# Weight sums on VectorE and by accumulating DMAs in the second feed-forward product

## The chip, the cores and the metric

The kernel runs on one core of a Trainium2 chip. The metric is the device time of one execution in microseconds (us). Five engines work side by side, each through its own queue of instructions in order: TensorE (PE in the profile, its weight loads PEld), VectorE (DVE), ScalarE (ACT), GpSimd (POOL) and SyncE (SP). SP does nothing here but issue DMA transfers. GpSimd issues some as well, among them the ones that add what they bring to what lies at their destination ("accumulating" transfers, `accum_op=OP.add`).

## The reference

One layer of a decoder over 2048 tokens of width 1024, in float32: a normalised input goes through one projection, two mixers (gated linear attention and dilated attention) and an output projection; then comes the part that matters here, a feed-forward block of width 4096 and a last normalisation.

```python
        mixed = jnp.concatenate([o_a, o_b], axis=-1).astype(h.dtype)
        h = h + jnp.einsum('bsm,md->bsd', mixed, w_out[l])

        nm = rmsnorm(h, mlp_norm_g[l])
        a = jnp.square(jax.nn.relu(jnp.einsum('bsd,df->bsf', nm, w_ff1[l])))
        h = h + jnp.einsum('bsf,fd->bsd', a, w_ff2[l])
    return rmsnorm(h, final_norm_g)
```

## The kernel before

**How a product is made.** A float32 product is made of three matmuls in a faster format: every operand is split into a high part, which ScalarE copies, and a low part, which VectorE subtracts (`split`, lines 485 to 487; the name of the split operand tells which one it is), and high x high, low x high and high x low are summed in PSUM (`mm3`, lines 141 to 144). One matmul is 128 x 128 by 512 columns.

**FF1**, the first feed-forward product, runs twice over 16 pairs of column blocks, first for one half of the tokens, then for the other. It uses a scheme of seven block products in place of eight (`product1`); a job is one of them, 224 in all, and `prep1` splits its weights two jobs ahead (`w1comb`). The token operands of the seven products (`hb`) are held split in SBUF. While the last seven jobs of the first half run (from job `first` = 105), those of the second half are brought in: `reload` loads 1 MB (tile `rb`, from `hTD`) and splits it in two halves, one per job or so (line 1606 is the call, the splits are line 486 on ScalarE and 487 on VectorE). The first two loads are issued at job 103, each later one when the first half of the load two before it has been split. The results go through a squared ReLU and, added and subtracted in many combinations, to memory (`actD`).

**FF2**, the second, is a scheme of 26 block products (`PRODUCTS`, lines 75 to 100). Each line of the table says which weight blocks make up its right operand, and after the bar to which output blocks the result is added. A product has four steps, one for each quarter of the operand, and a step is 24 matmuls; step n belongs to product n // 4. For its right operand the kernel keeps a weight state (`bs`, four quarters of 512 KB), which goes from product to product: "=" loads a block into the quarter (SP, line 1497), "+" and "-" add and subtract a block. `fetch_b(n)` brings the blocks to be added or subtracted into one of four half tiles (`rb`, SP, line 1487); `update_b(n)` adds them into the quarter (line 1499), the first on GpSimd, a second on VectorE. The four steps prepared while FF1 ends use VectorE for both. `prep_b(n)` then splits the quarter into one of three buffers (`cb`, line 486 on ScalarE, 487 on VectorE), and `prep_a(n)` does so for the activations (`ca`, loaded by SP as `ra`, 1 MB for two steps; products with sign -1 take lines 1458 and 1459 instead). Per step, the loop asks for the update four steps ahead, the fetch six ahead, both splits two ahead, then for the 24 matmuls.

A finished product's four PSUM banks are taken during the next product's steps (`taken`): the first contribution to an output block is copied by ScalarE, the others are added by VectorE (line 1556). The residual `h` is added to the output blocks by 16 accumulating transfers of 512 KB on GpSimd's queue (`begin`, line 1544, from `hD`; the table `RESIDUAL` says with which product). When a block row is complete, after products 20, 23, 24 and 25, `output` normalises its four tiles: ScalarE sums squares, GpSimd multiplies the first half by the weights g (line 1517), VectorE scales and multiplies the second half (line 1520), ScalarE scales the first (line 1521), and SP stores both.

**Order.** In FF1 and FF2 the framework's scheduler decides the order of instructions on each engine, from dependencies and its own estimates of time; on the chip every queue then runs in that order.

Of the kernel before, what the change touches and what calls it, by code (L numbers as in the profile page):

```python
# [13 lines left out]
AF = mybir.ActivationFunctionType  # L14
OP = mybir.AluOpType
# [101 lines left out]
def emit(tc, a, stop=99):  # L117
    nc = tc.nc
    V, A, G, T, SP = nc.vector, nc.scalar, nc.gpsimd, nc.tensor, nc.sync
# [6 lines left out]
    def ps(tag):  # L126
        return psum.tile([128, 512], F32, name="ps_" + tag, tag=tag, bufs=BANKS[tag])

    def slot(name, dt=F32, n=SLOT):

        return up.tile([128, SLOT], dt, name=name, tag="u", bufs=25)[:, :n]

    def view(t, shape):
        n = int(np.prod(shape))
        names = "abcd"[:len(shape)]
        return t[:, :n].rearrange(f"p ({' '.join(names)}) -> p {' '.join(names)}", **dict(zip(names, shape)))
# [29 lines left out]
    def stat(n=1):  # L166
        if stat_at[0] + n > 48:
            stat_at[0] = 0
        s = stats[:, stat_at[0]:stat_at[0] + n]
        stat_at[0] += n  # L170
        return s

    def rstd_of(ssq, width, n=1, bias=eps):
        r = stat(n)
        A.activation(r, ssq, AF.Ln, bias=bias, scale=1.0 / width)
        A.activation(r, r, AF.Exp, scale=-0.5)
        return r
# [46 lines left out]
    hTD = dram.tile([2, 7, 128, 4, 512], F32, name="hTD")  # L224
# [15 lines left out]
    CX, c11, c12, c21, c22, last = [t[:, GP * q:GP * q + GP] for t in acc for q in range(2)]  # L240
# [11 lines left out]
    order = (1, 2, 5, 6, 3, 4, 7)  # L252
# [4 lines left out]
    TF = {j: [slot(f"tb{j}", FR) for _ in range(2 if j < 7 else 1)] for j in order}  # L257
# [227 lines left out]
    def split(hi, lo, src):  # L485
        A.activation(hi, src, AF.Copy)  # L486
        V.tensor_tensor(lo, src, hi.bitcast(F32), op=OP.subtract)  # L487
# [109 lines left out]
    def reload(n):  # L597

        j, cs = order[n // 2], slice(1024 * (n % 2), 1024 * (n % 2) + 1024)
        t = (xp, bp)[n // 2 % 2][:, cs]  # L600
        SP.dma_start(t, nTD[j - 1].rearrange("p c s -> p (c s)")[:, cs])

        def rest():
            hi, lo = [v[:, cs] for v in TF[j]]
            tc.keep_in_program_order(A.activation(hi, t, AF.Copy))
            V.tensor_tensor(lo, t, hi.bitcast(F32), op=OP.subtract)
            if n + 4 < 14:
                back.append(reload(n + 4))

        return rest  # L610
# [121 lines left out]
    for at in range(7, len(jobs)):  # L732
        g = jobs[at][0]
# [419 lines left out]
    for pr in range(4):  # L1153
# [3 lines left out]
        for hh, br in seq:  # L1157
            b = Branch()
            b.h, b.br = 2 * pr + hh, br
            m = 4 if br == 2 else 2  # L1160
            first = len(units)
# [62 lines left out]
    rb, TF, TB = [slot("rb")], {}, {}  # L1224
# [53 lines left out]
    order = (1, 2, 6, 5, 7, 3, 4)  # L1278
# [10 lines left out]
    def prep1(at):  # L1289

        if at >= len(jobs1):
            return
        g, j = jobs1[at]
        if not combs1:
            combs1.extend(view(c[:, 1024 * q:], (2, 4, 128)) for c in [slot("w1comb", FR) for _ in range(2)]
                          for q in range(2))
        r = raw1[g % 2]
        (a11, a12), (a21, a22) = [[r[:, 4 * k:4 * k + 4, n * 128:n * 128 + 128] for k in range(2)] for n in range(2)]
        c = combs1[at % 4]
        split(c[:, 0], c[:, 1], {1: a11, 2: a12, 6: a11, 5: a21, 7: a11, 3: a12, 4: a22}[j])  # L1300
        if j == 1:
            V.tensor_tensor(a21, a21, a22, op=OP.add)
            V.tensor_tensor(a11, a21, a11, op=OP.subtract)
        if j == 2:
            V.tensor_tensor(a12, a12, a11, op=OP.subtract)
        if j == 6:
            V.tensor_tensor(a11, a22, a11, op=OP.subtract)
        if j == 4:
            load_w1(g + 2)
# [80 lines left out]
    def some_sums(n=3):  # L1390

        for _ in range(n):
            while sums1 and next(sums1[0], 0) == 0:
                sums1.pop(0)
# [5 lines left out]
    for at, t in enumerate(tiles):  # L1400
        u, m = nxt
# [7 lines left out]
        p = [ps("a"), ps("a")]  # L1409
        parts_ = 2 if at < 2 else 1  # L1410
        for q in range(parts_):
            for n in range(2):
                cs = slice(n * 512, n * 512 + 512)
# [20 lines left out]
    raw_a, comb_a, raw_b, comb_b, state, fin = [], [], [], [], [], {}  # L1434
# [5 lines left out]
    def load_a(n):  # L1440

        if n < 2 * NPH:
            p, k = divmod(n, 2)
            if len(raw_a) < 2:
                raw_a.append(view(slot("ra"), (4, 512)))
            SP.dma_start(raw_a[n % 2], actD[AT[p], :, 4 * k:4 * k + 4].rearrange("p q h s -> p q (h s)"))
# [16 lines left out]
    fetched = {}  # L1463

    def w2_part(n, k, m):

        first = 8 * (n % 4) + 2 * (k % 2) + k // 2
        return w2[:, first:first + 5:4, 512 * m:512 * m + 512]

    def state_of(n):  # L1470

        if len(state) < 2:
            state.extend(view(slot("bs"), (4, 512)) for _ in range(2))
        return state[n % 4 // 2][:, n % 2 * 2:n % 2 * 2 + 2]

    def fetch_b(n):

        if n >= LAST:
            return
        if not raw_b:  # L1480
            raw_b.extend(view(v[:, 1024 * e:], (2, 512)) for v in [slot("rb2") for _ in range(2)] for e in range(2))
        fetched[n] = []
        for op, k, m in PRODUCTS[n // 4][2]:
            if op != "=":
                v = raw_b[turns[0] % 4]
                turns[0] += 1
                SP.dma_start(v, w2_part(n, k, m))
                fetched[n].append((op, v))

    def update_b(n, engines=(G, V)):  # L1490

        if n >= LAST:
            return
        v = state_of(n)
        for op, k, m in PRODUCTS[n // 4][2]:
            if op == "=":
                SP.dma_start(v, w2_part(n, k, m))
        for e, (op, r) in enumerate(fetched.pop(n)):
            engines[e].tensor_tensor(v, v, r, op=OP.add if op == "+" else OP.subtract)  # L1499

# [9 lines left out]
    def output(C, row, i, last=False):  # L1510

        scr = fin["scr"][:, 512 * (i % 2):512 * (i % 2) + 512]
        ss, part = stat(2), stat()
        for n in range(2):
            A.activation(scr, C[n], AF.Square, accum_out=ss[:, n:n + 1])
            if n == 0:
                G.tensor_tensor(C[0], C[0], fin["g"][:, :512], op=OP.mult)
                A.activation(part, ss[:, 0:1], AF.Copy, bias=EPS, scale=1.0 / D)
        r = rstd_of(ss[:, 1:2], D, bias=part)
        V.scalar_tensor_tensor(C[1], C[1], r, fin["g"][:, 512:], op0=OP.mult, op1=OP.mult)  # L1520
        A.activation(C[0], C[0], AF.Copy, scale=r)
        SP.dma_start(out2[row:row + 128, 512:], C[1])
        (A if last else SP).dma_start(out2[row:row + 128, :512], C[0])

# [58 lines left out]

    first, parts_at = 7 * (NP - 1), {}
    for n in range(14):
        parts_at.setdefault(first + 1 + n * 4 // 5, []).append(n // 2)
    halves, begun = {}, set()
    for at in range(7, len(jobs1)):
        if at == first - 2:
            halves.update({n: reload(order[n], 1) for n in range(2)})  # L1590
        prep1(at + 2)
        some_sums()
        product1(at)
        for n in parts_at.get(at, ()):
            next(halves[n])
            if n in begun and n + 2 < 7:
                halves[n + 2] = reload(order[n + 2], 1)
            begun.add(n)
        n = at + 6 - len(jobs1)
        if n == 0:  # L1600
            load_a(0)
        if 0 <= n < 4:
            fetch_b(n)
            update_b(n, (V, V))
        if n == 3:
            load_a(1)
        if n in (3, 5):
            prep_b(n // 2 - 1)
            prep_a(n // 2 - 1)
            fetch_b(n // 2 + 3)  # L1610

    some_sums(99)
    held2 = [None, None]
# [1 line left out]
    for ph, (_, chained, _, _) in enumerate(PRODUCTS):  # L1615
        if not chained:
            held2[ph % 2] = [ps(t) for t in ("acdc", "adco")[ph % 2]]
        P = held2[ph % 2]
        for k in range(4):
            n = 4 * ph + k  # L1620
            update_b(n + 4)
            if n + 6 not in fetched:
                fetch_b(n + 6)
            prep_a(n + 2)
            prep_b(n + 2)
            if k == 1:
                begin(ph)
            if left:
                taken(ph - 1, k, left[k])
            if ph < NPH - 1 or k < 2:  # L1630
                for c in range(2):
                    for i in range(4):
                        mm2(P[i], n, c, i, not chained)
        left = P
# [60 lines left out]
```

## Time and profile before

| | |
|---|---|
| median of 3 runs | 2280.32 us (2277.76 to 2281.45) |
| profiled execution, own time | 2283.21 us |
| its span | 2281.4 us |
| mean granted TensorE clock | 0.994 |
| TensorE busy | 2249.2 us (99%) |
| VectorE busy | 1630.4 us (71%) |
| ScalarE busy | 1230.4 us (54%) |
| GpSimd busy | 544.3 us (24%) |
| FF2's first weight split | 1678.9 us from the span's start |

The profile is of one execution. A row of its groups gives source line, engine, operation, output<-input with partitions x elements and type, the count, then total busy time, mean duration in ns, and how long the engine was idle just before, with what ended most of that time. In a timeline the first two numbers are start and duration in us, and the bracket is the idle time before, with its releaser. A row for one tile gives minimum, median and maximum duration in ns and the first and last start.

### The profile page before, as it was taken

How to read it: one execution, taken by the hardware profiler on the slowest of the kernel's cores; microseconds unless marked ns; L12 is line 12 of the kernel's file. 1: busy time of each engine (PE TensorE's matmuls, PEld its weight loads, DVE VectorE, ACT ScalarE, POOL GpSimd, SP SyncE). 2: the span in 40 equal slices, each digit the busy share in tenths (PEclk: the TensorE clock that was granted, in tenths of full speed). 3: DMA queues.
4: the chain of work that ended last, by engine and by line, in shares of the span. 5: the costliest groups of instructions: out<-in, count | busy, mean ns of one | idle time of the engine just before them, and what ended most of it. 6: DMA issues, size and time to landing. Idle time of an engine off the chain costs nothing.

```text
span 2281.4 us, 35136 instructions
## 1 busy us (share of the span) xinstructions
PE 2249.2 (99%) x12508; PEld 1945.9 (85%) x12508; DVE 1630.4 (71%) x3065; ACT 1230.4 (54%) x2436; POOL 544.3 (24%) x482
## 2 busy tenths in 40 slices
PE   9999999999999999999999999999999999999998
PEld 8978998899999998888888887888888878888876
DVE  8788878766667676446777778777777577576778
ACT  6665436426877874234555556555555433333446
POOL 1210002024385672000000000000007562032465
PEclk9999999999999999999999999999999999999999
DMA  5458754776768864678544456555479988676775
GB/s 201 134 182 245 252 155 136 223 234 221 223 196 255 262 207 139 221 232 273 185 138 153 137 161 202 163 165 163 128 266 285 311 279 277 214 254 227 261 255 175
DMA packets 359920, 478.59 MB, mean 210 GB/s; under 512 B 19333, under 2 KB 268694, under 8 KB 347712
## 3 DMA queue, kind: packets, MB, share of 16 engines
q1 hardware_dynamic: 355246, 467.69, 63.6%
q0 software_dynamic: 4352, 8.39, 2.0%
q8 instruction: 98, 1.61, 0.3%
q14 instruction: 78, 0.64, 0.1%
q10 hardware_dynamic: 146, 0.27, 0.0%
HBM read 326.54 MB, written 154.44 MB: 211 GB/s over the span
## 4 chain that ended last, share of the span: by engine, by line
PE 84%; DMA 5%; POOL 3%; DVE 3%; issue 3%; ACT 2%; SPq 0%; POOLq 0%; ACTq 0%; DVEq 0%
PE ps_a L143 9%; PE ps_a L142 9%; PE ps_a L144 9%; PE ps_c L143 7%; PE ps_c L142 7%; PE ps_c L144 7%; PE ps_a L893 4%; PE ps_o L142 3%; PE ps_o L144 3%; PE ps_o L143 3%; PE ps_d L143 3%; PE ps_d L142 3%; PE ps_d L144 3%; PE ps_d L874 3%; PE ps_c L852 2%
## 5 line engine op out<-in xcount | busy, mean ns | idle before, releaser
L1499 POOL TENSOR_TENSOR bs<-bs,rb 128x1024 f32<-128x1024 f32 x72 | 217.7, 3031 | 1072.3 <-DMA actD<-ring 836.9
L486 ACT ACTIVATE cb<-bs 128x1024 fp32r<-128x1024 f32 x104 | 110.2, 1060 | 272.7 <-issue 116.2
L487 DVE TENSOR_TENSOR cb<-bs,cb 128x1024 fp32r<-128x1024 f32 x104 | 165.2, 1589 | 124.4 <-ACT cb L486 123.7
L487 DVE TENSOR_TENSOR w1comb<-w1raw,w1comb 128x512 fp32r<-128x512 f32 x224 | 153.8, 689 | 96.4 <-ACT w1comb L486 95.5
L486 ACT ACTIVATE w1comb<-w1raw 128x512 fp32r<-128x512 f32 x224 | 140.3, 628 | 81.6 <-PE ps_c L144 29.5
L865 ACT ACTIVATE pe<-pe,O 128x256 f32<-128x256 f32 (+1 forms) x384 | 156.5, 453 | 45.8 <-DVE O L864 42.3
L893 PE MATMUL ps_a<-v,pt 128*128 128x65 f32 x1200 | 178.5, 253 | 2.5 <-ACT pt L881 1.9
L893 PEld LDWEIGHTS ps_a<-v,pt 128*128 128x128 f32 x1200 | 175.4, 196 | 3.5 <-ACT pt L881 2.1
L874 PE MATMUL ps_d<-ident,pe 128*128 128x128 f32 x600 | 159.7, 279 | 0.0
L864 DVE CUSTOM_DVE_ANT_0 pe<-ps_c,nb 128x256 f32<-128x256 f32 (+1 forms) x384 | 126.3, 361 | 40.9 <-PE ps_d L874 18.3
L286 ACT ACTIVATE wcomb<-wraw 128x512 fp32r<-128x512 f32 (+2 forms) x119 | 90.0, 757 | 98.8 <-PE ps_a L143 34.5
L142 PE MATMUL ps_c<-hb,w1comb 128*128 128x512 f32 x336 | 131.0, 390 | 0.5 <-ACT xs L1371 0.5
L143 PE MATMUL ps_c<-hb,w1comb 128*128 128x512 f32 x336 | 130.9, 390 | 0.0
L144 PE MATMUL ps_c<-hb,w1comb 128*128 128x512 f32 x336 | 130.2, 390 | 0.0
L487 DVE TENSOR_TENSOR ca<-ra,ca 128x1024 fp32r<-128x1024 f32 x84 | 126.8, 1511 | 3.8 <-ACT ca L486 3.8
L142 PE MATMUL ps_c<-cb,ca 128*128 128x512 f32 x312 | 122.1, 391 | 0.0
L143 PE MATMUL ps_c<-cb,ca 128*128 128x512 f32 x312 | 122.0, 391 | 0.0
L144 PE MATMUL ps_c<-cb,ca 128*128 128x512 f32 x312 | 122.0, 391 | 0.0
L351 POOL TENSOR_TENSOR acc<-acc,misc 128x264 f32<-128x264 f32 (+1 forms) x32 | 38.7, 1221 | 313.1 <-DMA wraw<-w_in 200.3
L874 PEld LDWEIGHTS ps_d<-ident,pe 128*128 128x128 f32 x600 | 110.0, 187 | 0.1
L142 PE MATMUL ps_a<-wo,mT 128*128 128x512 f32 x256 | 101.4, 396 | 0.0
L1362 ACT ACTIVATE acc<-acc 128x512 f32<-128x512 f32 x96 | 60.7, 632 | 74.1 <-DVE acc L1381 44.0
(410 smaller groups left out, 7146.7 us busy)
## 6 DMA issues: line engine op xcount, KB each, us to landing
ra<-actD SPq DMA_DIRECT2D x52, 1024.0 KB, 7.3
actD<-ring SPq DMA_DIRECT2D x176, 256.0 KB, 2.5
rb<-w_ff SPq DMA_DIRECT2D x88, 512.0 KB, 6.1
bs<-w_ff SPq DMA_DIRECT2D x72, 512.0 KB, 6.1
w1raw<-w_ff SPq DMA_DIRECT2D x32, 1024.0 KB, 5.7
k<-kD SPq DMA_DIRECT2D x16, 1024.0 KB, 7.4
rb<-hTD SPq DMA_DIRECT2D x13, 1024.0 KB, 5.9
wraw<-w_in SPq DMA_DIRECT2D x48, 256.0 KB, 3.9
```

The costliest lines, as they stand in the source:

```text
L142: T.matmul(out, sh, mh, start=first, stop=False, **kw)
L143: T.matmul(out, sl, mh, start=False, stop=False, **kw)
L144: T.matmul(out, sh, ml, start=False, stop=last, **kw)
L286: A.activation(hi, src, AF.Copy, scale=sc)
L486: A.activation(hi, src, AF.Copy)
L487: V.tensor_tensor(lo, src, hi.bitcast(F32), op=OP.subtract)
L864: V.tensor_tensor_reduce(p, s, bias, scale=1.0, scalar=BIG, op0=OP.add, op1=OP.min, accum_out=nm)
L865: A.activation(p, p, AF.Exp, bias=nm, scale=-1.0)
L874: T.transpose(pb[:, i * 128:i * 128 + 128], src, ident)
L893: T.matmul(self.b.opsum[:, n % 4], self.pt[:, i * 128:i * 128 + 128], self.b.v[:, blk, cols], start=first, stop=last)
L1362: A.activation(v, v, AF.Relu)
L1499: engines[e].tensor_tensor(v, v, r, op=OP.add if op == "+" else OP.subtract)
```

## The change

1. `update_b` uses VectorE alone: no weight sum is left on GpSimd. From step 16 on, "+" blocks are not fetched into `rb` at all; an accumulating transfer on GpSimd's queue adds them from memory to the state. Of 88 sums, 72 on GpSimd and 16 on VectorE, 52 remain, all on VectorE (12 "+" of the first four products and 40 "-"), and 36 become accumulating transfers: four each in products 4, 6, 8, 9, 16, 18, 21, 23 and 25. SP issues 52 block fetches in place of 88; the 72 "=" loads stay. Where a line of the table has both, the accumulating transfer comes before the subtraction.
2. In `output`, for 15 of the 16 tiles the first half is scaled and multiplied by VectorE in one instruction, as the second half is, in place of GpSimd's product and ScalarE's scaling.
3. The reload for the second half of the tokens is cut into 14 pieces of 512 KB. Four are issued one job earlier than the first two loads were, and piece n + 4 is issued once piece n has been split.
4. In FF2 the update is asked for three steps ahead in place of four, and the fetch five in place of six; before the loop, three updates are made in place of four.

In the order that the scheduler makes, VectorE has 2851 instructions in place of 2799, ScalarE 1897 in place of 1909, GpSimd 227 in place of 274 and SP 842 in place of 873 (waits left out). GpSimd's queue then holds the residual transfers and the weight transfers in turn: the first two residual blocks, the transfers of steps 16 and 17, one of the next residual block, that of 18, and so on; those of steps 32 to 39 alternate with six residual transfers, and those of steps 64 and later have no residual transfers among them. On VectorE, after product 7, stand the splits of step 29, the sum of step 32 (which waits for its transfer), four PSUM additions, the sum of 33, the splits of 30 and 31, the sum of 34 and the splits of 32.

```diff
@@ -1481,13 +1481,13 @@
             raw_b.extend(view(v[:, 1024 * e:], (2, 512)) for v in [slot("rb2") for _ in range(2)] for e in range(2))
         fetched[n] = []
         for op, k, m in PRODUCTS[n // 4][2]:
-            if op != "=":
+            if op == "-" or op == "+" and n < 16:
                 v = raw_b[turns[0] % 4]
                 turns[0] += 1
                 SP.dma_start(v, w2_part(n, k, m))
                 fetched[n].append((op, v))
 
-    def update_b(n, engines=(G, V)):
+    def update_b(n, engines=(V, V)):
 
         if n >= LAST:
             return
@@ -1495,6 +1495,8 @@
         for op, k, m in PRODUCTS[n // 4][2]:
             if op == "=":
                 SP.dma_start(v, w2_part(n, k, m))
+            elif op == "+" and n >= 16:
+                G.dma_start(v, w2_part(n, k, m), accum_op=OP.add)
         for e, (op, r) in enumerate(fetched.pop(n)):
             engines[e].tensor_tensor(v, v, r, op=OP.add if op == "+" else OP.subtract)
 
@@ -1514,11 +1516,15 @@
         for n in range(2):
             A.activation(scr, C[n], AF.Square, accum_out=ss[:, n:n + 1])
             if n == 0:
-                G.tensor_tensor(C[0], C[0], fin["g"][:, :512], op=OP.mult)
+                if last:
+                    G.tensor_tensor(C[0], C[0], fin["g"][:, :512], op=OP.mult)
                 A.activation(part, ss[:, 0:1], AF.Copy, bias=EPS, scale=1.0 / D)
         r = rstd_of(ss[:, 1:2], D, bias=part)
         V.scalar_tensor_tensor(C[1], C[1], r, fin["g"][:, 512:], op0=OP.mult, op1=OP.mult)
-        A.activation(C[0], C[0], AF.Copy, scale=r)
+        if last:
+            A.activation(C[0], C[0], AF.Copy, scale=r)
+        else:
+            V.scalar_tensor_tensor(C[0], C[0], r, fin["g"][:, :512], op0=OP.mult, op1=OP.mult)
         SP.dma_start(out2[row:row + 128, 512:], C[1])
         (A if last else SP).dma_start(out2[row:row + 128, :512], C[0])
 
@@ -1583,31 +1589,40 @@
 
     first, parts_at = 7 * (NP - 1), {}
     for n in range(14):
-        parts_at.setdefault(first + 1 + n * 4 // 5, []).append(n // 2)
-    halves, begun = {}, set()
+        parts_at.setdefault(first + 1 + n * 4 // 5, []).append(n)
+    piece = lambda n: rb[n // 2 % 2][:, 1024 * (n % 2):1024 * (n % 2) + 1024]
+
+    def load_piece(n):
+
+        if n < 14:
+            SP.dma_start(piece(n), hTD[1, order[n // 2] - 1][:, 2 * (n % 2):2 * (n % 2) + 2].rearrange("p c s -> p (c s)"))
+
     for at in range(7, len(jobs1)):
-        if at == first - 2:
-            halves.update({n: reload(order[n], 1) for n in range(2)})
+        if at == first - 3:
+            for n in range(4):
+                load_piece(n)
         prep1(at + 2)
         some_sums()
         product1(at)
         for n in parts_at.get(at, ()):
-            next(halves[n])
-            if n in begun and n + 2 < 7:
-                halves[n + 2] = reload(order[n + 2], 1)
-            begun.add(n)
+            cs = slice(1024 * (n % 2), 1024 * (n % 2) + 1024)
+            split(*[v[:, cs] for v in TF[order[n // 2]]], piece(n))
+            load_piece(n + 4)
         n = at + 6 - len(jobs1)
         if n == 0:
             load_a(0)
-        if 0 <= n < 4:
+        if 0 <= n < 3:
             fetch_b(n)
             update_b(n, (V, V))
+        if n == 3:
+            fetch_b(n)
         if n == 3:
             load_a(1)
         if n in (3, 5):
             prep_b(n // 2 - 1)
             prep_a(n // 2 - 1)
-            fetch_b(n // 2 + 3)
+            if n == 3:
+                fetch_b(4)
 
     some_sums(99)
     held2 = [None, None]
@@ -1618,9 +1633,9 @@
         P = held2[ph % 2]
         for k in range(4):
             n = 4 * ph + k
-            update_b(n + 4)
-            if n + 6 not in fetched:
-                fetch_b(n + 6)
+            update_b(n + 3)
+            if n + 5 not in fetched:
+                fetch_b(n + 5)
             prep_a(n + 2)
             prep_b(n + 2)
             if k == 1:
```

## The prediction

> **What bounds the kernel now.** I read the page's engine totals first, then the costliest groups of the second feed-forward part (FF2, from 1680 us on).
>
> ```profile
> span 2281.4 us, 35136 instructions
> PE 2249.2 (99%) x12508; PEld 1945.9 (85%) x12508; DVE 1630.4 (71%) x3065; ACT 1230.4 (54%) x2436; POOL 544.3 (24%) x482
> q1 hardware_dynamic: 355246, 467.69, 63.6%
> q0 software_dynamic: 4352, 8.39, 2.0%
> L1499 POOL TENSOR_TENSOR bs<-bs,rb 128x1024 f32<-128x1024 f32 x72 | 217.7, 3031 | 1072.3 <-DMA actD<-ring 836.9
> L487 DVE TENSOR_TENSOR cb<-bs,cb 128x1024 fp32r<-128x1024 f32 x104 | 165.2, 1589 | 124.4 <-ACT cb L486 123.7
> L487 DVE TENSOR_TENSOR ca<-ra,ca 128x1024 fp32r<-128x1024 f32 x84 | 126.8, 1511 | 3.8 <-ACT ca L486 3.8
> ```
>
> TensorE is busy for 99% of the span and the change leaves its matmuls alone, so a gain can only come from stretches where TensorE lacks work or runs on a lowered clock. I looked for them by counting matmuls in windows of 50 us. The columns are busy time and instructions of PE, PEld, DVE, ACT and POOL, then the granted clock, the DMA engines' share and GB/s.
>
> ```profile
> 1350.00:1400.00 50.00, 44.73 (x185) 36.07 (x184) 44.06 (x72) 34.40 (x53) 0.00 (x0) 0.94 0.67 217
> 1400.00:1450.00 50.00, 50.00 (x220) 41.37 (x219) 37.90 (x78) 27.37 (x47) 0.00 (x0) 0.99 0.53 161
> 1700.00:1750.00 50.00, 50.00 (x222) 41.46 (x221) 38.52 (x41) 24.48 (x30) 29.59 (x12) 1.00 0.85 270
> 1750.00:1800.00 50.00, 50.00 (x223) 41.42 (x222) 29.76 (x24) 26.50 (x35) 31.63 (x14) 1.00 1.08 306
> 1800.00:1850.00 50.00, 48.88 (x212) 39.16 (x211) 29.71 (x24) 20.06 (x22) 27.49 (x9) 1.00 0.84 289
> 1850.00:1900.00 50.00, 49.05 (x213) 39.34 (x212) 44.75 (x40) 18.08 (x18) 29.51 (x13) 1.00 0.90 274
> 2150.00:2200.00 50.00, 45.74 (x191) 37.28 (x190) 47.92 (x32) 24.16 (x48) 37.44 (x14) 0.93 0.78 268
> 2200.00:2250.00 50.00, 48.66 (x215) 39.99 (x213) 40.33 (x32) 27.46 (x56) 33.42 (x14) 1.00 0.63 205
> ```
>
> A full window holds 222 matmuls, so one takes 50/222 = 0.2252 us and a step of 24 takes 5.4 us. Missing matmuls times 0.2252 give the loss: 37 and 2 at the half change, 8.3 + 0.5 = 8.8 us; 10 and 9 in 1800 to 1900, 4.3 us; 31 and 7 in 2150 to 2250, 8.6 us. These 21.7 us are the most that the change can return.
>
> **What makes each loss.** At the half change (line 1606) ScalarE, in its order, waits for the reload of the second half's operands, and TensorE waits behind it for a copy out of PSUM.
>
> ```profile
> 1370.36 1.06 ACT L486 ACTIVATE hb<-rb 128x1024 fp32r<-128x1024 f32 x1 [1.66 <-DMA rb<-hTD]
> 1393.40 1.06 ACT L486 ACTIVATE hb<-rb 128x1024 fp32r<-128x1024 f32 x1 [2.86 <-DMA rb<-hTD]
> 1373.42 0.50 PE L142 MATMUL ps_d<-hb,w1comb 128*128 128x512 f32 x1 [2.68 <-ACT xs L1371]
> 1380.00:1390.00 10.00, 10.00 (x46) 8.29 (x45) 10.00 (x16) 9.74 (x16) 0.00 (x0) 1.00 0.84 269
> 1390.00:1400.00 10.00, 7.41 (x29) 5.66 (x28) 10.00 (x18) 5.59 (x10) 0.00 (x0) 0.89 0.51 175
> ```
>
> In 1800 to 1900 the weight state goes round a loop on two engines: VectorE splits it, GpSimd adds a block, VectorE subtracts the next, VectorE splits again.
>
> ```profile
> 1839.10 1.22 DVE L487 TENSOR_TENSOR cb<-bs,cb 128x1024 fp32r<-128x1024 f32 x1
> 1840.40 3.32 POOL L1499 TENSOR_TENSOR bs<-bs,rb 128x1024 f32<-128x1024 f32 x1 [2.47 <-DVE cb L487]
> 1843.75 1.23 DVE L1499 TENSOR_TENSOR bs<-bs,rb 128x1024 f32<-128x1024 f32 x1 [2.29 <-POOL bs L1499]
> 1844.89 1.22 DVE L487 TENSOR_TENSOR cb<-bs,cb 128x1024 fp32r<-128x1024 f32 x1
> ```
>
> One turn is 1844.89 - 1839.10 = 5.79 us against the 5.4 of a step, so TensorE falls behind. After 2150 the outputs come on top, and VectorE's operations stretch to 3.4 us beside GpSimd's, where the row above shows 1.22:
>
> ```profile
> 2173.64 3.43 DVE L487 TENSOR_TENSOR cb<-bs,cb 128x1024 fp32r<-128x1024 f32 x1
> 2176.99 3.36 DVE L487 TENSOR_TENSOR ca<-ra,ca 128x1024 fp32r<-128x1024 f32 x1
> 2180.41 0.80 PE L143 MATMUL ps_a<-cb,ca 128*128 128x512 f32 x1 [4.26 <-DVE ca L487]
> 2180.00:2185.00 5.00, 4.59 (x11) 3.63 (x12) 5.00 (x4) 1.06 (x1) 3.23 (x2) 0.50 1.00 372
> ```
>
> TensorE stands for 4.26 us and then gets half its clock, 11 matmuls in 5 us.
>
> **VectorE's balance.** It takes over work, and is relieved of the stretching. Medians and means of the groups:
>
> ```profile
> L487 DVE TENSOR_TENSOR cb<-bs,cb x104: 1208/1226/3598, 1682.3 to 2262.5; 128x1024 fp32r<-128x1024 f32 x104
> L487 DVE TENSOR_TENSOR ca<-ra,ca x84: 1210/1218/3428, 1684.4 to 2263.7; 128x1024 fp32r<-128x1024 f32 x84
> L1459 DVE SCALAR_TENSOR_TENSOR ca<-ra,ca 128x1024 fp32r<-128x1024 f32 x20 | 31.3, 1566 | 0.7 <-ACT ca L1458 0.7
> L1520 DVE SCALAR_TENSOR_TENSOR sum<-sum,stats,gf 128x512 f32<-128x512 f32 x16 | 24.3, 1540 | 1.0 <-ACT stats L176 0.9
> L1520 DVE SCALAR_TENSOR_TENSOR sum<-sum,stats,gf x16: 739/1770/2895, 2163.0 to 2276.0; 128x512 f32<-128x512 f32 x16
> ```
>
> Relief, if every one returns to its undisturbed time: 104 x (1.589 - 1.226) = 37.8; 84 x (1.511 - 1.218) = 24.6; 20 x (1.566 - 1.218) = 7.0; 16 x (1.540 - 0.740) = 12.8; together 82 us. Added: VectorE did 16 of the 88 sums and now does 52, 36 x 1.226 = 44.1; 15 of 16 output tiles scale their first half on it, 15 x 0.74 = 11.1; together 55. VectorE ends 27 us lighter.
>
> **The sum, part by part.**
>
> Loop of products 5 to 7: the GpSimd sum leaves it. Two splits and two sums on VectorE are 4 x 1.22 = 4.9 us, under 5.4: -4.3. Bounds: 0 (VectorE's other work fills the 0.5 left) and -4.3.
>
> Outputs (lines 1517, 1520, 1521): 15 GpSimd products of 1.7 us and the weight sums beside them go, so nothing stretches VectorE. One product's four steps then ask of it 8 splits, 8 sums, 4 PSUM additions of 0.68 and 8 scalings, 16 x 1.22 + 2.7 + 5.9 = 28 us at the heaviest against 21.8 us, while about two steps of operands (three buffers) lie ahead, 10.8 us: no stall. I take -8.6, the whole loss; bounds 0 and -8.6. ScalarE loses 15 scalings; it isn't late there.
>
> Reload in 14 pieces, four in flight: begun one job earlier and half as long, it should take the two ScalarE waits (1.66 and 2.86 us) and the TensorE stall of 2.68 away. But VectorE is busy for 20 us of 20 in 1380 to 1400 and that part stays, so -5 of 8.8. Bounds: -8.8, and +2 if seven more issues on SP delay the neighbouring loads (about one wait of the size above). If the reload comes in time, VectorE's splits are late next.
>
> Earliest loads (fetch and sum one step later, the fourth sum after the loop): they move behind the loads of FF1's end, where TensorE has its full 222; lookahead of three steps is 16 us against a landing of 6.1. 0; without that cover about one landing.
>
> GpSimd's issues: 36 of about 1.2 us are 43 us in place of 217.7 us of sums, but in one queue with the 16 residual transfers (line 1544), whose waits they now share. SP issues 36 block loads fewer.
>
> The accumulating DMAs have no price in this trace for weights. The nearest rows are the residual's, of the same size and queue, but with short rows of HBM, and then the plain loads:
>
> ```profile
> L1544 POOL DMA_DIRECT2D sum<-hD x16: 1175/1205/2145, 1739.7 to 1959.3; - x16
> DMA to landing us min/median/max: 6.5/11.7/20.3
> sum<-hD POOLq DMA_DIRECT2D x4, 512.0 KB, 10.7
> bs<-w_ff SPq DMA_DIRECT2D x72, 512.0 KB, 6.1
> ```
>
> The third line is for 1850 to 1890 alone. I take L = 10.7 us to landing, from the place where the first ones run, and 6.1 and 20.3 as ends. Who waits: the split of the step waits for the quarter, and where a "-" block follows, VectorE's sum waits in order, with PSUM additions and the splits of earlier steps queued behind it. The tightest place is product 8 (steps 32 to 35): its quarters are free only when product 7's splits are made. Split 29 ends about 2.4 us into step 27; then come the transfer, the sum and two splits (3.7 us), and step 30 starts 16.3 us after step 27: L up to 10.2 costs nothing. The transfer of step 34 goes out one turn later and behind two residual transfers, so it may last 8.4. At 10.7 the cost is 0.5 + 2.3 = 2.8 us; at 6.1 nothing; at 20.3, 10.1 + 11.9 = 22 and two dips of the clock as after the 4.26-us stall (11 matmuls where 22 fit, 2.5 us each), 27. The accumulates that follow a "=" load in the same quarter (products 6, 16, 18, 21, 25) have some 10 us to spare beyond 6.1 + 6.5, so they pay only toward the upper end. I take +2.8.
>
> DMA engines: q0's 2.0% for 8.39 MB is 45.6 us of 16 engines, 2.85 us for 512 KB; q1's 63.6% for 467.69 MB gives 1.63. Each accumulate costs 1.22 us more, and sixteen of them fall in 1700 to 1900, +19.5. The shares there sum to 0.85 + 1.08 + 0.84 + 0.90, 183.5 us of 200, with the new ones 203. TensorE kept 223 matmuls at a share of 1.08, so I take +1; ends 0 and 19.5.
>
> The Trainium skill ("DMA: Bandwidth & Descriptors", section "Anatomy of one DMA — SWDGE (gpsimd) path") gives a DMA from GpSimd's queue 2.0 us and its bytes by 436 GB/s, an estimate of 3.2 us here. The rows above, 6.5 to 20.3, disagree; by the page product 8 would cost nothing and the sum would be 2.8 us lower. The skill's "SBUF — State Buffer", section "Who interferes with whom", speaks against the change: such a transfer's descriptors starve while VectorE runs in a mode that takes the shared ports, though it says that tensor_tensor has no such mode; the issue row, 1205 at the median with 2145 at most, shows little of it, and that one's excess on L would add some 2 us.
>
> Sum: 2281.4 - 4.3 - 8.6 - 5 + 2.8 + 1 = 2267.3 us of span. The profiled execution's time, 2283.21, is 1.8 over its span, and the median of the runs, 2280.32, is 1.1 under that span. In terms of the median: 2266.
>
> **Rivals.**
> *Late accumulates.* L is near 20 under weight traffic, and VectorE's queue stands behind it at product 8 and again at 6, 16, 18, 21 and 25. For it: the 20.3 row, the dense stretch. Against: most weight rows are plain, long transfers, and L = 10.7 in that very stretch. Price 27 - 2.8 = 24 more: 2290, slower. It decides against the change from L of about 16 (product 8 then costs 13.4 us and some clock, against gains of 18).
> *The DMA engines are the bound in 1700 to 1900.* The 19.5 us of extra work delay the loads there by about half, +10: 2276. For: 183.5 of 200. Against: 223 matmuls at 1.08.
> *VectorE is the bound, or the reload stays late.* Its 28 us per product at the outputs outrun the lead, and the half change keeps its loss since VectorE was full there: only 4.3 comes back less 3.8, 2280, no change.
>
> **How the numbers follow.** Forecast 0.57, with its own range 2259 (every loss returned and no cost) to 2274 (the half change returns nothing and L costs two more); late accumulates 0.22; DMA engines 0.11; VectorE or reload 0.10. A measurement of this kernel tells about 0.2%, 4.6 us. Faster: 0.57 + most of 0.11 = 0.66. Same: 0.10 and a little of the others, 0.12. Slower: 0.22. The range runs from 2259 to 2289, to just short of the late rival's centre, leaving out its longer half, 0.11, and 0.05 below.
>
> **What will show it.** Right: 222 matmuls in each window of 1350 to 1400, 1800 to 1900 and 2150 to 2250; splits at 1.22 us throughout; accumulates landing in 6 to 11 us; no PE wait above 1 us after 1800. Wrong: PE waits at steps 30 and 31 with "DMA bs<-w_ff" ahead of VectorE's sum; shares above 1 with fewer matmuls in 1700 to 1900; TensorE's stall near 1373 still there.

## The result and the profile after

| | before | after |
|---|---|---|
| median of 5 runs each | 2280.32 us | 2292.07 us |
| ratio of the runs, 95% interval | | 1.0051 [1.0041, 1.0062] |
| profiled execution, own time | 2283.21 us | 2292.94 us |
| its span | 2281.4 us | 2290.9 us |

The change made the kernel 0.5% slower, where 0.6% faster was forecast. The engine totals, queues and groups of the profile after:

```profile
span 2290.9 us, 35029 instructions
PE 2249.7 (98%) x12508; PEld 1944.8 (85%) x12508; DVE 1597.5 (70%) x3116; ACT 1220.3 (53%) x2421; POOL 347.8 (15%) x431
q0 software_dynamic: 14144, 27.27, 6.6%
L487 DVE TENSOR_TENSOR cb<-bs,cb 128x1024 fp32r<-128x1024 f32 x104 | 127.1, 1222 | 120.2 <-ACT cb L486 120.2
L1501 DVE TENSOR_TENSOR bs<-bs,rb 128x1024 f32<-128x1024 f32 x52 | 63.6, 1222 | 71.7 <-DMA bs<-w_ff 67.9
```

VectorE is 33 us lighter and its splits take 1222 ns in place of 1589, as worked out. But the last row shows a new thing: VectorE's remaining sums stand still for 67.9 us, waiting for transfers into the weight state. The windows say where TensorE pays (columns as before):

```profile
1350.00:1400.00 50.00, 47.45 (x206) 38.05 (x205) 45.50 (x78) 36.41 (x56) 0.00 (x0) 1.00 0.66 214
1800.00:1850.00 50.00, 47.20 (x195) 38.14 (x194) 30.63 (x29) 17.13 (x18) 7.22 (x6) 0.93 0.94 295
1850.00:1900.00 50.00, 42.05 (x173) 33.90 (x172) 25.76 (x26) 14.42 (x15) 12.13 (x10) 0.93 1.00 245
1900.00:1950.00 50.00, 47.43 (x202) 38.73 (x201) 31.32 (x32) 16.07 (x16) 0.00 (x0) 0.97 0.74 232
2100.00:2150.00 50.00, 48.32 (x214) 39.71 (x213) 30.70 (x33) 18.68 (x19) 0.00 (x0) 1.00 0.69 214
2150.00:2200.00 50.00, 48.17 (x211) 39.05 (x210) 37.60 (x43) 22.63 (x44) 7.22 (x6) 1.00 0.95 286
```

Against 222 in a full window, 16 are missing at the half change (before: 39 with the window behind it) and 11 in 2150 to 2200 (before: 38 with the window behind it): these two gained. In 1800 to 1950 it is 27 + 49 + 20 = 96, that is 21.6 us, where before it was 19. This stretch holds the steps of products 6 to 9. Pieces of the timeline, of SP, POOL, ACT, VectorE (DVE) and PE, show how it happens at product 6 and, behind the dots, at product 8:

```profile
1797.15 2.64 SPq L1497 DMA_DIRECT2D bs<-w_ff  x2
1809.95 2.53 POOL L1499 DMA_DIRECT2D bs<-w_ff  x2 [26.76 <-DMA bs<-w_ff]
1820.66 1.06 ACT L486 ACTIVATE cb<-bs 128x1024 fp32r<-128x1024 f32 x1 [11.73 <-PE ps_o L144]
1822.71 0.80 PE L142 MATMUL ps_a<-cb,ca 128*128 128x512 f32 x1 [2.15 <-ACT ca L1458]
...
1846.36 1.20 POOL L1499 DMA_DIRECT2D bs<-w_ff  x1 [1.07 <-DVE cb L487]
1858.39 1.23 DVE L1501 TENSOR_TENSOR bs<-bs,rb 128x1024 f32<-128x1024 f32 x1
1861.94 0.50 PE L143 MATMUL ps_a<-cb,ca 128*128 128x512 f32 x1 [2.33 <-DVE ca L487]
1861.05 1.20 POOL L1499 DMA_DIRECT2D bs<-w_ff  x1 [1.21 <-DVE cb L487]
1873.81 1.23 DVE L1501 TENSOR_TENSOR bs<-bs,rb 128x1024 f32<-128x1024 f32 x1 [9.66 <-DMA bs<-w_ff]
1878.74 0.80 PE L143 MATMUL ps_a<-cb,ca 128*128 128x512 f32 x1 [5.62 <-DVE ca L487]
```

At product 6 the first "=" loads are issued from 1797.15 on. The accumulating transfers go out at 1809.95, when the loads of the same quarters have landed, and the first one takes 10.6 us to land, by a view below; the split follows at 1820.66, and TensorE stands for 2.15 us. (The split's bracket names TensorE, whose last matmul before the stall ended at about the same time.) At product 8 the transfer of step 33 goes out at 1846.36, the sum of step 33 follows at 1858.39, the splits of step 30 stand behind it, and TensorE waits 2.33 us for them. The transfer of step 34 goes out at 1861.05; VectorE waits 9.66 us for it, with the splits of step 32 behind it, and TensorE stands for 5.62 us. The view of line 1499 gives the accumulates' durations of issue on GpSimd (ns) and their landings:

```profile
L1499 POOL DMA_DIRECT2D bs<-w_ff x36: 1194/1203/1345, 1746.9 to 2253.5; - x36
DMA to landing us min/median/max: 7.7/11.0/23.8
```

The views of the DMA issues from 1846 to 1848 and from 1860.5 to 1862 give, in their last column, the landings of the transfers of steps 33 and 34:

```profile
bs<-w_ff POOLq DMA_DIRECT2D x1, 512.0 KB, 12.0
bs<-w_ff POOLq DMA_DIRECT2D x1, 512.0 KB, 12.7
```

### The profile page after: what moved, and what is told of

Its sections match the earlier page's. It is cut to its first block, busy times and chain, and to the rows that moved or that the text cites. A ratio compares the mean times of both kernels' runs of the same rounds, so it can differ in the third digit from the quotient of the medians.

```text
span 2290.9 us, 35029 instructions
## 1 busy us (share of the span) xinstructions
PE 2249.7 (98%) x12508; PEld 1944.8 (85%) x12508; DVE 1597.5 (70%) x3116; ACT 1220.3 (53%) x2421; POOL 347.8 (15%) x431
## 3 DMA queue, kind: packets, MB, share of 16 engines
q0 software_dynamic: 14144, 27.27, 6.6%
## 4 chain that ended last, share of the span: by engine, by line
PE 81%; DMA 9%; issue 4%; DVE 3%; ACT 1%; POOL 1%; SPq 0%; POOLq 0%; DVEq 0%; ACTq 0%
PE ps_a L143 9%; PE ps_a L144 9%; PE ps_a L142 9%; PE ps_c L143 7%; PE ps_c L142 7%; PE ps_c L144 7%; DMA bs<-w_ff 6%; PE ps_a L893 4%; PE ps_o L144 3%; PE ps_o L143 3%; PE ps_o L142 3%; PE ps_d L143 3%; PE ps_d L142 3%; PE ps_d L144 3%; PE ps_d L874 3%
## 5 line engine op out<-in xcount | busy, mean ns | idle before, releaser
L487 DVE TENSOR_TENSOR cb<-bs,cb 128x1024 fp32r<-128x1024 f32 x104 | 127.1, 1222 | 120.2 <-ACT cb L486 120.2
L1550 POOL DMA_DIRECT2D sum<-hD x16 | 19.6, 1283 | 966.7 <-ACT sum L1559 869.7
L1501 DVE TENSOR_TENSOR bs<-bs,rb 128x1024 f32<-128x1024 f32 x52 | 63.6, 1222 | 71.7 <-DMA bs<-w_ff 67.9
L487 DVE TENSOR_TENSOR ca<-ra,ca 128x1024 fp32r<-128x1024 f32 x84 | 102.3, 1219 | 7.9 <-ACT ca L486 7.9
```

## The experiments

Each kernel was timed in rounds against the kernel before on the same chip; ratios are to that, with 95% intervals. The runs of one kernel spread over 2 to 14 us, and a profile shows one of them, so the verdicts rest on the ratios, and the windows say only where.

**No accumulating transfers.** From the changed kernel:

```diff
-            if op == "-" or op == "+" and n < 16:
+            if op != "=":
...
-            elif op == "+" and n >= 16:
-                G.dma_start(v, w2_part(n, k, m), accum_op=OP.add)
```

> The changed kernel without its accumulating transfers: all 88 blocks are fetched and summed on VectorE. In the changed kernel's windows 96 matmuls (21.6 us) are missing in 1800 to 1950 and 21 (4.7 us) in 2000 to 2200. Theory A (the accumulates start only once the quarter is free and land late, and the splits wait): both go, 2292 - 26 = about 2266. Theory B (VectorE's sums are too many): 36 more sums, 44 us of VectorE, 2292 or above.

Measured: 2283.99 us, 1.0018 [1.0006, 1.0030]. Both theories fail in part. Most of the loss of 1800 to 1950 goes (220, 209 and 216 matmuls), but 2000 to 2150 is worse than in either kernel:

```profile
2000.00:2050.00 50.00, 46.12 (x193) 36.69 (x192) 32.13 (x33) 15.80 (x16) 0.00 (x0) 0.97 0.72 240
2050.00:2100.00 50.00, 48.59 (x215) 39.91 (x214) 29.25 (x31) 17.51 (x19) 0.00 (x0) 1.00 0.69 225
2100.00:2150.00 50.00, 46.06 (x201) 37.18 (x200) 30.04 (x32) 17.86 (x18) 0.00 (x0) 1.00 0.66 216
```

VectorE is not full there, 32 of 50 us. Its waits from 1690 us on, in us, times and longest, name something else, and in 2000 to 2150 TensorE waits for its splits:

```profile
DVE bs L1499 <- DMA bs<-w_ff: 96.6, 28, 8.2
DVE bs L1499 <- DMA bs<-w_ff: 52.1, 14, 5.8
PE ps_a L143 <- DVE ca L487: 9.2, 7, 2.6
```

The second and third lines are for 2000 to 2150 alone. In the kernel before, the wait for the "=" load stood in GpSimd's queue, from 1690 us on:

```profile
POOL bs L1499 <- DMA bs<-w_ff: 193.4, 25, 36.9
```

Now the sum that waits for it stands in VectorE's, and the splits behind it wait as well. I call this theory E; it is tried below.

**Accumulates only late, or only early.** As the changed kernel, with the bound 16 replaced:

```diff
-            if op == "-" or op == "+" and n < 16:
+            if op == "-" or op == "+" and n < 64:
...
-            elif op == "+" and n >= 16:
+            elif op == "+" and n >= 64:
```

> Accumulates only from step 64 on (20 of 36), the early 16 blocks fetched and summed on VectorE. Theory A: 21.6 us come back, about 2270, with 2000 to 2200 as in the changed kernel. Theory B: 2292 or above.

Measured: 2274.49 us, 0.9971 [0.9961, 0.9982], faster than both kernels. For the other half the condition is 16 <= n < 64:

> Accumulates only in steps 16 to 39, the other 20 blocks fetched and summed on VectorE. Theory A: the 21.6 us of 1800 to 1950 stay, at most the 4.7 us behind go, about 2288. Theory B: 2292 or above, with VectorE late after 2150.

Measured: 2300.0 us, 1.0085 [1.0073, 1.0097]. The number is theory B's, and 2150 to 2200 is late, with 193 matmuls. But VectorE is busy for only 40 of 50 us there and waits 9.7 us for "=" loads, so it is not the count of its sums alone. So the same instruction pays in one place and costs in the other. Early accumulates add 0.0080 (changed kernel less acc_late) or 0.0067 (acc_early less no_acc), 15 to 18 us. Late ones take 0.0034 or 0.0047 away, 8 to 11 us: they put the wait for the "=" load back into GpSimd's queue. Acc_late has 221, 222 and 220 matmuls in 2000 to 2150, and VectorE's wait there falls from 52.1 us (no_acc) to 23.1.

**The longer lookahead again.** From the changed kernel:

```diff
-            update_b(n + 3)
-            if n + 5 not in fetched:
-                fetch_b(n + 5)
+            update_b(n + 4)
+            if n + 6 not in fetched:
+                fetch_b(n + 6)
...
```

> The changed kernel with update and fetch asked for one step earlier again (four and six). Theory C (the shorter lookahead makes the accumulates late): they are issued a step, 5.4 us, earlier, most of the 21.6 us comes back, about 2272. Theory A: the quarter is freed by the split of its last use, which the lookahead does not move, so within 4 us of 2292.

Measured: 2288.16 us, 1.0035 [1.0024, 1.0047]: 4 us better than the changed kernel, and 1850 to 1900 has 165 matmuls, no more than the 173. The lookahead is worth those 4 us at most and isn't the cause of the loss.

**The same transfers without the adding.** This kernel leaves out the 36 additions.

```diff
-                G.dma_start(v, w2_part(n, k, m), accum_op=OP.add)
+                G.dma_start(v, w2_part(n, k, m))
```

> The changed kernel with its 36 accumulating transfers as plain ones from the same queue, at the same points: they overwrite the quarter, so the 36 additions are left out. Theory D (the adding itself makes them late): they land in 5 to 6 us like SP's, in place of 11.0, the 21.6 us of 1800 to 1950 go, about 2272. Theory A (they start late, behind the split and the = load, and GpSimd's queue lands slowly): landing stays at 9 us or more, at most a third comes back, 2285 to 2292.

Measured: 2271.48 us, 0.9965 [0.9952, 0.9978]; 1800 to 1950 has 223, 215 and 218 matmuls. The same queue, the same bytes and the same waits ahead of the issue cost almost nothing once the transfer doesn't add. Theory A, as I had put it, falls: it isn't the late start alone, nor GpSimd's queue. The queue's row of the page (packets, MB, share of the engines), and then the view of line 1499:

```profile
q0 software_dynamic: 9536, 27.27, 4.4%
```

```profile
L1499 POOL DMA_DIRECT2D bs<-w_ff x36: 722/723/908, 1749.3 to 2233.3; - x36
DMA to landing us min/median/max: 4.4/7.3/15.4
```

It lands in 7.3 us in place of 11.0, is issued in 723 ns in place of 1203, and takes (4.4% of 2271.1 - 2.0% of 2281.4)/36 = 1.51 us of the 16 engines, where the adding one takes (6.6% of 2290.9 - 45.6)/36 = 2.93. Whether a shorter issue, a lighter load on the engines or the adding itself shortens the landing most, this run doesn't separate. The Trainium skill ("DMA: Bandwidth & Descriptors", section "Anatomy of one DMA — SWDGE (gpsimd) path") would have 3.2 us for a transfer of this size from GpSimd's queue, an estimate from its 2.0 us and 436 GB/s; even the fastest plain one here took 4.4, so the measurement decides.

**Without product 8, and without products 6 and 8.** Steps 32 to 35, then steps 24 to 27 and 32 to 39 (so product 9's four as well), are fetched and summed on VectorE, the rest as in the changed kernel:

```diff
-            elif op == "+" and n >= 16:
+            elif op == "+" and (16 <= n < 32 or n >= 36):
...
+            elif op == "+" and (16 <= n < 24 or n >= 40):
```

> The changed kernel with the blocks of product 8 (steps 32 to 35) fetched and summed on VectorE, the other 32 still accumulated. If product 8 is the tightest place, as the prediction had it, the 49 matmuls missing in 1850 to 1900 and the 20 behind come back to some 15, that is 12 us: 2280. If every early accumulate is as bad, a quarter of the 16 us between acc_early and no_acc: 2288.

Measured: 2279.18 us, 0.9996 [0.9987, 1.0004]. Product 8 alone is worth 0.0055, 12.5 us; 1850 to 1900 is full again. The windows:

```profile
1800.00:1850.00 50.00, 46.17 (x191) 37.41 (x190) 32.83 (x32) 17.89 (x20) 4.81 (x4) 0.93 0.95 290
1850.00:1900.00 50.00, 50.00 (x223) 41.38 (x222) 34.56 (x35) 18.10 (x18) 9.69 (x8) 1.00 1.01 290
```

The DMA engines' share in the full window is 1.01, so their load is not what stopped TensorE there. What stays, 31 missing in the first row, is in part product 6: the next kernel still misses 13 there. The next kernel's expectation speaks of product 9 as accumulated; as run, its blocks were summed on VectorE.

> The changed kernel with the blocks of products 6 and 8 fetched and summed on VectorE, those of 4, 9 and all from step 64 on accumulated. If products 6 and 8 alone are too tight for a landing of 11 us, as acc_late is within 3 us: 2272 to 2277. If accumulates in the dense stretch cost by their load on the DMA engines, half of the 17.6 us between the changed kernel and acc_late stays: 2283.

Measured: 2275.92 us, 0.9982 [0.9974, 0.9991], within 2.5 us of acc_late: product 4's early accumulates do no harm that is clear of the noise (the profile of acc_not68 misses 21 matmuls in 1800 to 1950, that of acc_late 8). Against acc_not8 the ratio falls by 0.0014, 3.2 us, for products 6 and 9 together.

**The reload alone, and acc_late without it.** Their edit is the reload part of the change's diff, put into the kernel before (reload_only), or taken out of acc_late (late_no_reload):

```diff
+    def load_piece(n):
+        if n < 14:
+            SP.dma_start(piece(n), hTD[1, order[n // 2] - 1][...])
...
-        if at == first - 2:
-            halves.update({n: reload(order[n], 1) for n in range(2)})
+        if at == first - 3:
+            for n in range(4):
+                load_piece(n)
...
```

> The kernel before with the reload in 14 pieces and nothing else. 39 matmuls were missing at the half change before, 16 after: 23 x 0.2252 = -5.2, about 2276 against 2281. If what stays is only moved to later stages, 2281.

Measured: 2279.49 us, 0.9998 [0.9990, 1.0007].

> acc_late with the reload as in the kernel before. If the reload in pieces is worth the 4 to 5 us that its window shows: 2279. If it is worth nothing, as the times of reload_only say: 2274.5.

Measured: 2275.96 us, 0.9980 [0.9970, 0.9990], against 0.9971 with the pieces. The reload in pieces is worth between nothing and about 3 us. The windows agree: of the kernels with the old reload, the first two windows miss 39, 31, 30 and 25 matmuls, of those with the pieces 16 to 23. The profile of the kernel before that the prediction read is of an execution 2.9 us over the median, and it shows the largest loss of them all.

**The outputs alone.** The kernel before with the change's edit of `output`:

```diff
-                G.tensor_tensor(C[0], C[0], fin["g"][:, :512], op=OP.mult)
+                if last:
+                    G.tensor_tensor(C[0], C[0], fin["g"][:, :512], op=OP.mult)
...
+            V.scalar_tensor_tensor(C[0], C[0], r, fin["g"][:, :512], op0=OP.mult, op1=OP.mult)
```

> The kernel before with the outputs' first half on VectorE and nothing else; the weight sums stay on GpSimd. If GpSimd's products at the outputs make the stall near 2180, most of 8.6 us goes: 2273. If the weight sums on GpSimd stretch VectorE there by themselves, VectorE only has more to do: 2281 or a little above.

Measured: 2277.86 us, 0.9993 [0.9985, 1.0002]. The big loss stays, 192 matmuls in 2150 to 2200, with GpSimd's weight sums still there. The groups of that window show the splits as before:

```profile
L487 DVE TENSOR_TENSOR cb<-bs,cb 128x1024 fp32r<-128x1024 f32 x9 | 20.3, 2253 | 6.7 <-ACT cb L486 6.7
```

It is the weight sums that stretch the splits there: with the sums gone the same group takes 1220 ns (changed kernel), and it takes 1218 in vv_only, below, where the outputs' products are still on GpSimd. Those products stretch VectorE as well, but there are only four in the window. In vv_only a sum on VectorE took 2.17 us beside two of them, where the others take 1.22:

```profile
2169.23 2.55 POOL L1517 TENSOR_TENSOR sum<-sum,gf 128x512 f32<-128x512 f32 x2 [212.96 <-ACT gf L1515]
2170.70 2.17 DVE L1499 TENSOR_TENSOR bs<-bs,rb 128x1024 f32<-128x1024 f32 x1
```

The Trainium skill's "SBUF — State Buffer", section "Who interferes with whom", says so of such pairs of instructions: tensor_tensor with both inputs in SBUF contends with GpSimd's reads. 1220 against 2253 ns agrees.

**All sums on VectorE alone, and late first sums on GpSimd.** The first is the kernel before, the second no_acc:

```diff
-    def update_b(n, engines=(G, V)):
+    def update_b(n, engines=(V, V)):
...
-            engines[e].tensor_tensor(v, v, r, op=OP.add if op == "+" else OP.subtract)
+            (G if e == 0 and n >= 64 else V).tensor_tensor(v, v, r, op=OP.add if op == "+" else OP.subtract)
```

> The kernel before with every weight sum on VectorE and nothing else. By the prediction's own steps (the 5.79 us loop and the stretching go): 2280 - 4.3 - 5 = 2271. Theory E: these gains are eaten by VectorE's waits for = loads, as in no_acc, 2280 to 2285.

Measured: 2286.92 us, 1.0030 [1.0019, 1.0041]. Moving the sums to VectorE makes the kernel slower by itself, 6.8 us, at the old lookahead; VectorE waits 95.2 us for "=" loads, and 2000 to 2150 has 205, 217 and 200 matmuls. In 2150 to 2200 the splits are no longer stretched, and still only 195 matmuls run: VectorE waits 9.3 us for "=" loads there.

> No accumulating transfers as in no_acc, but from step 64 on the first block of a step is added by GpSimd, as before. Theory E (in no_acc VectorE's queue stands at sums that wait for the = load, with later splits behind them; GpSimd's queue or a transfer took that wait elsewhere): the 57 matmuls missing in 2000 to 2150 come back, -12.8 us, and the stretched splits at the outputs cost some 4 again, 2284 - 9 = 2275. Rival (the shorter lookahead makes those loads late): 2284 or above.

Measured: 2277.6 us, 0.9991 [0.9981, 1.0002]. The stretch is full again with the short lookahead, and the outputs stall as before. The windows:

```profile
2000.00:2050.00 50.00, 49.79 (x220) 40.92 (x219) 37.15 (x30) 18.47 (x19) 11.47 (x4) 1.00 0.75 256
2100.00:2150.00 50.00, 50.00 (x222) 41.43 (x221) 34.62 (x30) 17.56 (x20) 22.83 (x8) 1.00 0.70 241
2150.00:2200.00 50.00, 46.44 (x192) 37.54 (x191) 46.08 (x38) 23.55 (x44) 31.20 (x10) 0.93 0.80 279
```

Its VectorE's waits from 1690 us on, and then, for 2000 to 2150, those of VectorE and TensorE, as above:

```profile
DVE bs L1499 <- DMA bs<-w_ff: 38.1, 13, 7.4
DVE bs L1499 <- DMA bs<-w_ff: 7.8, 2, 4.2
PE ps_a L143 <- DVE ca L487: 0.2, 1, 0.2
```

Theory E stands: in 2000 to 2150 VectorE's wait falls from 52.1 to 7.8 us and TensorE's wait for its splits from 9.2 to 0.2, and the place recovers where the wait was taken off VectorE's queue. (The sums themselves left VectorE too, but it had room, 32 of 50 us.) The total from 1690 us on decides nothing by itself: acc_late still has 57.9 us of it and is no slower than this kernel.

## Why the prediction was wrong

The time came out as the first rival had it (2290 against 2292.07 measured). Its mechanism is right at products 8 and 6, but without its condition: L didn't have to be near 20. At products 16, 18, 21 and 25, which it named too, it is wrong, since the late accumulates paid. So the agreement of the number is partly luck: the rival set 27 us of cost against 18 of gains, where the runs show 15 to 18 us for the early accumulates, and smaller gains.

*The accumulates, +2.8 us: the step that failed.* The price of the transfer was nearly right, 10.7 taken and 11.0 measured, and 2.85 us of the engines against 2.93. The place was right too: product 8. What was mis-sized is how far L lies beyond the place's limits. At product 8 it was 12.0 (step 33) and 12.7 (step 34); by the step's own limits that is (12.0 - 10.2) + (12.7 - 8.4) = 6.1 us. TensorE stood for 2.33 + 5.62 = 8.0 us where the step had 0.5 + 2.3, and the clock fell to 0.93 in that window, another 3.5 us (0.07 of its 50), which the step charged only at its upper end; acc_not8 measured 12.5 for the whole. And 7.3 us, the plain transfer's landing, lies inside both limits: plain_pool lost little there. At a place whose limits lie under the median, the upper half of the landings should have been weighed as well.

*"The accumulates that follow a "=" load have some 10 us to spare": wrong at product 6.* Two landings in a row were priced at quiet values, 6.1 and 6.5, which with the 10 to spare makes 22.6 us from the issue of the "=" load to the split. By the DMA issues from 1795 to 1825 they took 10.3 and 10.8 at the median, which would still have fitted. In the product's first step they took 12.3 and 10.6 (issues from 1797 to 1798 and from 1809.5 to 1811), and the split came 1820.66 - 1797.15 = 23.5 us after the load's issue. In 1800 to 1850, 27 matmuls are missing; 13 are still missing there in acc_not68, and the times give 3.2 us for products 6 and 9.

```profile
bs<-w_ff SPq DMA_DIRECT2D x4, 512.0 KB, 10.3
bs<-w_ff POOLq DMA_DIRECT2D x4, 512.0 KB, 10.8
bs<-w_ff SPq DMA_DIRECT2D x1, 512.0 KB, 12.3
bs<-w_ff POOLq DMA_DIRECT2D x1, 512.0 KB, 10.6
```

*VectorE 27 us lighter: right (33), but it was the wrong measure.* The step counted busy time. It didn't ask what a sum on VectorE waits for when the state's "=" load is late, which is the wait that GpSimd's queue had held. Vv_only puts the price of the bare move at 6.8 us, gains included.

*The loop of products 5 to 7, -4.3.* The 5.79 us turn is gone in vv_only, where 1800 to 1900 has 214 and 219 matmuls against 222, so 11 are missing in place of 19: 1.8 us came of it.

*Outputs, -8.6.* Right in the changed kernel in direction, with 11 missing in 2150 to 2250 in place of 38: 6.1 us. As to the cause it is right in part. With the weight sums left on GpSimd the edit of the outputs is not enough: output_only and sums_g_late both miss 29 there. But an end of the stretching is not enough either: with the sums on VectorE 26 (vv_only), 19 (no_acc) and 29 (acc_early) are missing, and VectorE waits for "=" loads. The place fills up, to within 12, only in the kernels whose late blocks come by transfers from GpSimd's queue. (The step's 21.8 us for four steps is 21.6 by its own 5.4, which changes nothing.)

*Reload, -5.* Too large: 0 to 3 us. The step read its loss from one execution, and of all the profiles that one shows the largest loss at this place.

*DMA engines, +1.* No loss by load alone was found: in acc_not8 a share of 1.01 stood beside 223 matmuls. Whether the load lengthened the landings stays open.

## What to carry to other kernels

When work moves to another engine, move its waits on paper as well: ask which semaphore it waits for, and which instructions of that in-order queue stand behind it. A helper engine that is slow and mostly idle can be worth its place because it waits. An accumulating DMA takes the wait off a compute queue, but can't start before the buffer that it adds to is free, so use it where the gap between the buffer coming free and its next use is well over its landing under load: here late in FF2 (0.9971 [0.9961, 0.9982]), not in the dense stretch.

## What the runs showed of the hardware

An accumulating transfer of 512 KB from HBM into SBUF costs 1.5 to 2 times a plain one from the same queue, each at its median in its own kernel: 2.93 against 1.51 us of the 16 DMA engines, 1203 against 723 ns of issue, 11.0 against 7.3 us to landing, and (14144 - 4352)/36 = 272 packets against (9536 - 4352)/36 = 144.
